# Three units in place of two at the opening of each stage, and the norm's factor a unit later

## The chip, the cores and the metric

The kernel runs on one core of a Trainium2 chip, as one launch. The metric is device time in microseconds (us), lower is better. Before the change it took 1333.68 us, the median of three runs (1332.94 to 1336.54).

## The reference

A sequence of 256 positions with 1024 features goes through two blocks. The first has a conditioned feed-forward layer (SwiGLU, 2816 wide), a mixer (a gated convolution and a two-directional gated delta rule with 8 heads) and a second SwiGLU. The second has differential attention, a squared-ReLU MLP (4096 wide), an mLSTM layer and another MLP. Each of these layers begins with the same step, and that is where the change is made:

```
def _rmsnorm(x, w):
    xf = x.astype(jnp.float32)
    y = xf * lax.rsqrt(jnp.mean(xf * xf, axis=-1, keepdims=True) + EPS)
    return (y * w.astype(jnp.float32)).astype(x.dtype)
...
        u = _modulate(_rmsnorm(h, norm_mix[l]), sh2, sc2)
        h = h + g2 * _hybrid_mixer(u, w_in[l], ...)
...
        h = h + mix.astype(h.dtype)
        h = h + sqrelu_mlp(rmsnorm(h, mlp_norm[layer]), mlp_w1[layer], mlp_w2[layer]).astype(h.dtype)
```

The norm's factor (one number per position) can be multiplied into a product behind the matrix product, so the product can start before the factor is known.

## The kernel before

**Units.** Activations lie features by positions: x and h are eight tiles of 128 x 256 (k = 0 to 7). Every float32 product is made as three: a value is split into a rounded part (hi) and a rest (lo), and hi*hi, hi*lo and lo*hi are added (`mm3`, lines 429 to 431: weights hi by x hi, weights hi by x lo, weights lo by x hi). 128 columns of weights are a *unit*: 8 tiles by 3, 24 matmuls (`unit_cols`). A stage is a row of such units, each with an accumulator in one of PSUM's eight banks: four have the tag "up", four the tag "acc", and each tag is handed out in turn.

**Weights.** `Stream` loads two units at a time from memory ("raw"). A unit is prepared by a cast on ScalarE (ACT), "whi", line 320, and a subtraction on VectorE (DVE), "wlo", line 323 (a few on GpSimd). It lies in a buffer until the last matmul that reads it; there are three such buffers in ffn1's end and the mixer (`NSLOT`), and five in all later stages (`wider`). `unit` takes the next prepared unit, prepares others into what buffers are free, and then lets side work go one step further: `flush` runs what was put off with `later`, `tick` takes one step in each generator of `self.side`.

**A stage's opening.** The last product of a stage updates h from four acc banks, pair of tiles by pair (lines 874 and 878); `x_late` makes the x of the next stage from it (hi on ACT, line 739, lo on DVE, line 743). As the pairs come one by one, `unit_first` opens two units together: for each pair the hi products of both (lines 466 and 467), then the lo products of both (line 470). Their accumulators are two acc banks. In five of the six openings an acc bank has been taken for a square of h in between (line 644), so these are the second and third bank that h is updated from.

**The norm.** `group` is called behind each unit with its evacuation. The squares are summed by matmuls (line 672) inside the unit that follows the second group (`SUM`), and DVE makes the factor from that by a row of small operations (lines 675 and 523 to 537). At the fourth group (`SPREAD`) TensorE spreads it over the partitions (line 699), ACT copies it ("rs", line 713), and all evacuations held until then run on DVE: line 1642 in the mixer ("zs", with "lbias", line 772), 945 to 957 in ffn2, 1197 in attention, 997 and 999 in the MLPs ("t", "r"), 1943 in the mLSTM ("raw"). Until then the accumulators of those units stay in their banks.

**The shifted x.** The mixer's first eight units and ffn2's first ten use an x without the conditioning's shift and without the factor ("xw"). Meanwhile `x_full`, a side job, makes the full x for the rest: per tile a multiplication on DVE ("xt", line 757), ACT's addition of the shift ("xh", line 760) and the rest on DVE ("xl", line 764). It begins when the factor is there and takes a group of tiles at each tick: pairs in the mixer; one, one and then pairs in ffn2.

**The mLSTM.** Behind the fourth unit the gates' small product (lines 2020 to 2023) takes an up bank of its own, and `ml_gates` multiplies it by the factor (lines 1808 and 1809). In attention `cores` starts the first pair of heads when its q and k are there.

What stands in the program in which order on each engine follows from the order in which this code is run; nothing reorders it later.

Of the kernel before, what the change touches and what calls it, by code (L numbers as in the profile page):

```python
# [25 lines left out]
NFF = DFF // P  # L26
NFF2 = DFF2 // P
NLATE2 = 10
SUM, SPREAD = 2, 4
NLATE = 8  # L30
SX = S + 2
FIRST = ((0, 4), (4, 8))
# [357 lines left out]
class Kern:  # L390
# [62 lines left out]

    def unit_first(self, name, x):

        w = [self.st.next(name, 0) for i in range(2)]
        self.flush()
        self.tick()
        n = x[0].shape[-1]
        pss = [self.acc2().rearrange("p a b -> p (a b)")[:, :n] for i in range(2)]  # L460
        t = self.nc.tensor
        for j in range(KT // 2):
            ks = [(k, slice(k * P, (k + 1) * P)) for k in (2 * j, 2 * j + 1)]
            for (wh, wl), ps in zip(w, pss):
                for k, s in ks:
                    t.matmul(ps, lhsT=wh[:, s], rhs=x[0][:, k], start=k == 0, stop=False, skip_group_check=True)  # L466
                    t.matmul(ps, lhsT=wl[:, s], rhs=x[0][:, k], start=False, stop=False, skip_group_check=True)  # L467
            for (wh, wl), ps in zip(w, pss):
                for k, s in ks:
                    t.matmul(ps, lhsT=wh[:, s], rhs=x[1][:, k], start=False, stop=k == KT - 1, skip_group_check=True)  # L470
        return pss
# [426 lines left out]
    def swiglu(self, nm, gate_v, late, wide=None, after_wide=None, first=None):  # L898

        nc = self.nc  # L900
        up, dn = f"w_{nm}_up", f"w_{nm}_down"
        g = {}
        with ExitStack() as es:
            fp = es.enter_context(self.tc.tile_pool(name=nm, bufs=2))
            if first is None:
                self.down_start()

            def product(n, a, b):
                gf = fp.tile([P, S], F32, tag="gf", name="gf", bufs=4)
                a(gf)  # L910
                b(gf)
                gh = fp.tile([P, S], F32R, tag="gh", name="gh", bufs=8 if first else 6)
                gl = fp.tile([P, S], F32R, tag="gl", name="gl", bufs=8 if first else 6)
                self.split(gf, gh, gl)
                g[n] = (gh, gl)

            def silu(ps):
                sa = fp.tile([P, S], F32, tag="sa", name="sa", bufs=3)
                nc.scalar.activation(sa, ps, AF.Silu)  # L919
                return sa  # L920

            def whole(n, sa, ps):
                product(n, lambda gf: None, lambda gf: nc.vector.tensor_tensor(gf, ps, sa, op=ALU.mult))  # L923

            n0 = 0
            if first is not None:
                n0 = NFIRST
                self.first_products(lambda n, a, b: whole(n, silu(a), b))
                first.close()
                self.st.widen_until(lambda nm, n: es.enter_context(self.tc.tile_pool(name=nm, bufs=n)), self.st.nfirst)  # L930
                self.down_start()
                for n in range(0, NFIRST - 3, 2):
                    self.down(dn, None, n == 0, False, [g.pop(n), g.pop(n + 1)])
            for n in range(n0, NFF):
                if wide is not None and 2 * n < NLATE2:
                    if n == 0:
                        pa, pb = self.unit_first(up, wide)
                    else:
                        pa = self.up(SX)
                        self.unit_cols(pa, up, wide)  # L940
                    sa = fp.tile([P, S], F32, tag="sa", name="sa", bufs=3)

                    def gate_a(pa=pa, sa=sa):
                        t = fp.tile([P, S], F32, tag="ta", name="ta", bufs=2)
                        nc.vector.tensor_tensor(t, pa[:, :S], self.rs, op=ALU.mult)
                        nc.scalar.activation(sa, t, AF.Silu, bias=self.late_bias(pa))
                    self.group(gate_a)
                    if n > 0:
                        pb = self.up(SX)
                        self.unit_cols(pb, up, wide)  # L950

                    def gate_b(pb=pb, sa=sa, n=n):
                        def a(gf):
                            nc.vector.tensor_tensor(gf, pb[:, :S], self.rs, op=ALU.mult)

                        def b(gf):
                            nc.vector.scalar_tensor_tensor(gf, gf, self.late_bias(pb), sa, op0=ALU.add, op1=ALU.mult)
                        product(n, a, b)
                    if 2 * n + 2 == NLATE2:
                        self.flush()  # L960
                    self.group(gate_b)
                    if 2 * n + 2 == NLATE2:
                        after_wide()
                else:
                    x = (self.xh, self.xl)
                    ps = self.up()
                    self.unit_cols(ps, up, x)
                    sa = silu(ps)
                    ps = self.up()
                    self.unit_cols(ps, up, x)  # L970
                    whole(n, sa, ps)
                if n % 2 == 1 and n >= 3:
                    self.down(dn, None, n == 3 and n0 == 0, False, [g.pop(n - 3), g.pop(n - 2)])
            gate = self.small.tile([P, KT], F32, tag="gate", name="gate")
            nc.vector.tensor_scalar(gate, self.mod(gate_v), 0.5, None, op0=ALU.mult)
            self.down(dn, None, False, True, [g.pop(NFF - 2), g.pop(NFF - 1)], self.end_step(gate, late()))

    def mlp(self, l, late):
# [4 lines left out]
        with ExitStack() as es:  # L983
            fp = es.enter_context(self.tc.tile_pool(name=f"mlp{l}", bufs=2))
            self.late()
            started = False
            first = self.unit_first(up, x)
            for n in range(NFF2):
                if n < 2:
                    ps = first[n]  # L990
                else:
                    ps = self.up()
                    self.unit_cols(ps, up, x)

                def evac(n=n, src=ps):
                    t = fp.tile([P, S], F32, tag="t", name="t")
                    nc.vector.tensor_tensor(t, src, self.rs, op=ALU.mult)  # L997
                    r = fp.tile([P, S], F32, tag="r", name="r", bufs=6)
                    nc.vector.scalar_tensor_tensor(r, t, 0.0, t, op0=ALU.max, op1=ALU.mult)
                    gh = fp.tile([P, S], F32R, tag="gh", name="gh", bufs=10)  # L1000
                    gl = fp.tile([P, S], F32R, tag="gl", name="gl", bufs=10)
                    self.split(r, gh, gl)
                    g[n] = (gh, gl)
                self.group(evac)
                if n % 2 == 1 and n >= 7:
                    if not started:
                        self.down_start()
                    self.down(dn, None, not started, False, [g.pop(n - 7), g.pop(n - 6)])
                    started = True
            for n in (NFF2 - 6, NFF2 - 4):  # L1010
                self.down(dn, None, False, False, [g.pop(n), g.pop(n + 1)])
            self.down(dn, None, False, True, [g.pop(NFF2 - 2), g.pop(NFF2 - 1)], self.end_step(None, late()))
# [148 lines left out]
    def attention(self, late):  # L1161
        nc = self.nc
        x = (self.xh, self.xl)
        with ExitStack() as es:
# [13 lines left out]

            def cores():
                for hp in range(4):  # L1180
                    while not waiting:
                        yield
                    self.side.append(self.attn_core(*waiting.popleft(), bank))
                    for _ in range(APART):
# [436 lines left out]
    def mixer(self, wide, wide_es, late):  # L1621
        nc = self.nc
        nm = "w_in"
        with ExitStack() as es:
# [4 lines left out]
            self.eps = mp.tile([P, 1], F32, name="eps")  # L1629
            nc.vector.memset(self.eps, EPS)  # L1630
            self.late()
            self.side.append(self.x_full(self.gain_mix, self.mod(3), ((0, 1), (2, 3), (4, 5), (6, 7))))
            first = self.unit_first(nm, wide)
            for n in range(NLATE):
                if n < 2:
                    ps = first[n]
                else:
                    ps = self.up(SX)
                    self.unit_cols(ps, nm, wide)
# [159 lines left out]
    def ml_gates(self, ps):  # L1799
# [5 lines left out]
        ax = mp.tile([4, S], F32, name="gax")  # L1805
        z = mp.tile([4, S], F32, name="gz")
        b_if = self.vec("b_if")
        v.tensor_tensor(gi, ps[0:4], self.rs[0:4], op=ALU.mult)
        v.tensor_tensor(gf, ps[32:36], self.rs[32:36], op=ALU.mult)
        v.tensor_scalar(gi, gi, b_if[0:4, 0:1], None, op0=ALU.add)  # L1810
# [117 lines left out]
    def mlstm(self, late):  # L1928
# [3 lines left out]
        with ExitStack() as es:  # L1932
# [77 lines left out]
            first = self.unit_first(nm, x)  # L2010
            for n in range(8):
                h, i = divmod(n, 2)
                if n < 2:
                    ps = first[n]
                else:
                    ps = self.up()
# [60 lines left out]
    def run(self):  # L2077
# [107 lines left out]
        for i, name in enumerate(st):  # L2185
# [10 lines left out]
                self.mixer(self.xw, wes, late)  # L2196
            elif name == "ffn2":
                self.late()
                self.side.append(self.x_full(self.gain_mix, self.mod(6), ((0,), (1,), (2, 3), (4, 5), (6, 7))))

                def after_wide():
                    wes.close()
# [87 lines left out]
```

## Time and profile before

| | |
|---|---|
| runs of the kernel | 1333.68 us (1332.94, 1333.68, 1336.54) |
| the profiled execution's own time | 1331.56 us |
| its span, first to last instruction | 1329.7 us |
| mean granted TensorE clock | 0.991 of full speed |
| busy: TensorE, its weight loads, DVE, ACT, GpSimd | 98%, 96%, 73%, 50%, 4% |
| waits of TensorE at the openings (line 466) | 2.4 us in 5 waits |

PE is TensorE's matmuls, PEld its weight loads, SP the engine that issues the weight loads from memory. A row of a timeline gives the start in us from the span's start, the length in us, the engine, the line in the kernel, the operation, out<-in by the program's names, the shape, and how many in a row were merged; at the end in brackets the idle time in front and what ended it. Matmuls are pipelined: one lasts 0.28 us, and the next starts 0.12 us after it. The openings lie at 209.4 (mixer), 526.5 (ffn2), 718.3 (attention), 835.3 (first MLP), 1019.7 (mLSTM) and 1132.3 us (second MLP).

### The profile page before, as it was taken

Reading aid. Unit: us, or ns where it says so; the run is one execution under the profiler, and the core shown is the slowest. Engines: PE = TensorE matmul, PEld = TensorE weight load, DVE = VectorE, ACT = ScalarE, POOL = GpSimd, SP = SyncE. Lnnn points to the kernel's source line nnn. Section 1 sums busy time; section 2 is a strip of 40 time slices with the busy share of each in tenths; the row PEclk is TensorE's granted clock in tenths of the full one; section 3 lists DMA queues with packets and bytes.
Section 4 is the critical chain, followed back from the end, with each engine's and each line's share of the span. In section 5 each row is a group of like instructions: output and inputs, shape, how many; then the busy total and the mean of one; then the engine's idle time right before and its main releaser. Section 6 shows DMA issues by size and latency. Waiting matters only on the chain.

```text
span 1329.7 us, 26472 instructions
## 1 busy us (share of the span) xinstructions
PE 1297.0 (98%) x11058; PEld 1280.2 (96%) x11058; DVE 975.8 (73%) x1831; ACT 666.8 (50%) x1096; POOL 53.1 (4%) x42
## 2 busy tenths in 40 slices
PE   8999999989999989999999999999999999999997
PEld 7999999989999989999999999999999999999997
DVE  7997768789997586966556986965667957966654
ACT  3544445657545345634445566644445654644442
POOL 0000000233020000010000000000000000000000
PEclk8999999999999989999999999999999999999998
DMA  9998862444444364587554444455554435455550
GB/s 374 345 363 311 308 254 101 158 162 156 159 133 158 130 243 164 181 294 266 188 179 145 159 156 129 167 192 187 191 191 160 154 132 188 160 183 177 186 186 32
DMA packets 36680, 255.98 MB, mean 193 GB/s; under 512 B 4336, under 2 KB 4600, under 8 KB 6096
## 3 DMA queue, kind: packets, MB, share of 16 engines
q1 hardware_dynamic: 35136, 251.47, 53.1%
q0 software_dynamic: 560, 1.44, 0.4%
q8 instruction: 86, 1.41, 0.4%
q10 hardware_dynamic: 864, 1.38, 0.3%
q14 instruction: 34, 0.28, 0.1%
HBM read 253.03 MB, written 1.25 MB: 191 GB/s over the span
## 4 chain that ended last, share of the span: by engine, by line
PE 84%; DVE 13%; issue 1%; ACT 1%; DMA 1%; SPq 0%; DVEq 0%; ACTq 0%
PE up L429 16%; PE up L431 16%; PE up L430 15%; PE acc L430 9%; PE acc L429 9%; PE acc L431 9%; DVE wlo L323 3%; DVE raw L553 2%; PE acc L466 1%; PE acc L470 1%; PE acc L1567 1%; PE acc L467 1%; DVE tmp L1450 1%; DVE x L1452 1%; DMA vecs<-in_vecs 1%
## 5 line engine op out<-in xcount | busy, mean ns | idle before, releaser
L320 ACT CAST whi<-raw 128x1024 fp32r<-128x1024 f32 x404 | 420.5, 1047 | 417.8 <-PE up L430 172.6
L323 DVE TENSOR_TENSOR wlo<-raw,whi 128x1024 fp32r<-128x1024 f32 x390 | 474.0, 1225 | 61.0 <-ACT whi L320 59.5
L429 PE MATMUL up<-xh,whi 128*128 128x256 f32 x1744 | 498.7, 286 | 0.0
L431 PE MATMUL up<-xh,wlo 128*128 128x256 f32 x1744 | 492.8, 283 | 2.0 <-DVE wlo L323 2.0
L430 PE MATMUL up<-xl,whi 128*128 128x256 f32 x1744 | 492.6, 282 | 0.0
L431 PEld LDWEIGHTS up<-xh,wlo 128*128 128x128 f32 x1744 | 333.2, 191 | 2.9 <-DVE wlo L323 2.8
L429 PEld LDWEIGHTS up<-xh,whi 128*128 128x128 f32 x1744 | 334.4, 192 | 1.4
L430 PEld LDWEIGHTS up<-xl,whi 128*128 128x128 f32 x1744 | 333.3, 191 | 0.6 <-DVE xl L764 0.2
L429 PE MATMUL acc<-gh,whi 128*128 128x256 f32 x864 | 244.0, 282 | 0.0
L431 PE MATMUL acc<-gh,wlo 128*128 128x256 f32 x864 | 243.9, 282 | 0.0
L430 PE MATMUL acc<-gl,whi 128*128 128x256 f32 x864 | 243.9, 282 | 0.0
L429 PEld LDWEIGHTS acc<-gh,whi 128*128 128x128 f32 x864 | 165.9, 192 | 0.6 <-issue 0.6
L430 PEld LDWEIGHTS acc<-gl,whi 128*128 128x128 f32 x864 | 164.6, 191 | 0.0
L431 PEld LDWEIGHTS acc<-gh,wlo 128*128 128x128 f32 x864 | 164.6, 191 | 0.0
L997 DVE TENSOR_TENSOR t<-up,rs 128x256 f32<-128x256 f32 x60 | 25.4, 423 | 102.0 <-PE up L431 102.0
L553 DVE SCALAR_TENSOR_TENSOR raw<-raw,crow 128x1024 f32<-128x1024 f32 x72 | 87.9, 1249 | 3.8 <-DMA raw<-in_stream 3.8
L923 DVE TENSOR_TENSOR gf<-up,sa 128x256 f32<-128x256 f32 x35 | 14.6, 423 | 70.6 <-PE up L431 70.6
L323 POOL TENSOR_TENSOR wlo<-raw,whi 128x1024 fp32r<-128x1024 f32 x14 | 34.5, 2463 | 286.3 <-ACT whi L320 286.3
L919 ACT ACTIVATE sa<-up 128x256 f32<-128x256 f32 x35 | 13.1, 382 | 48.6 <-PE up L431 45.1
L429 PE MATMUL up<-whi,xh 128*128 128x256 f32 x128 | 37.3, 291 | 0.2 <-DVE raw L1943 0.2
L429 PE MATMUL acc<-yh,whi 128*128 128x256 f32 x128 | 36.2, 283 | 0.0
L430 PE MATMUL up<-wlo,xh 128*128 128x256 f32 x128 | 36.0, 281 | 0.0
(490 smaller groups left out, 1842.8 us busy)
## 6 DMA issues: line engine op xcount, KB each, us to landing
raw<-in_stream SPq DMA_DIRECT2D x238, 1024.0 KB, 4.9
h<-in_x SPq DMA_DIRECT2D x2, 512.0 KB, 4.7
bias<-bdram POOLq DMA_DIRECT2D x8, 128.0 KB, 6.0
out_h<-h SPq DMA_DIRECT2D x2, 256.0 KB, 2.7
out_h<-h ACTq DMA_DIRECT2D x2, 256.0 KB, 2.9
consts<-in_consts ACTq DMA_DIRECT2D x1, 384.0 KB, 7.7
vecs<-in_vecs SPq DMA_DIRECT2D x1, 312.0 KB, 7.5
wg<-in_w_g ACTq DMA_DIRECT2D x1, 256.0 KB, 2.6
```

Of the source, the lines that this page charges most:

```text
L320: nc.scalar.copy(hi[:, :n], raw)
L323: self.lows.append(lambda: eng.tensor_tensor(lo[:, :n], raw, hi[:, :n].bitcast(F32), op=ALU.subtract))
L429: t.matmul(ps, lhsT=wh, rhs=xh, start=start, stop=False, skip_group_check=True)
L430: t.matmul(ps, lhsT=wh, rhs=xl, start=False, stop=False, skip_group_check=True)
L431: t.matmul(ps, lhsT=wl, rhs=xh, start=False, stop=stop, skip_group_check=True)
L466: t.matmul(ps, lhsT=wh[:, s], rhs=x[0][:, k], start=k == 0, stop=False, skip_group_check=True)
L467: t.matmul(ps, lhsT=wl[:, s], rhs=x[0][:, k], start=False, stop=False, skip_group_check=True)
L470: t.matmul(ps, lhsT=wh[:, s], rhs=x[1][:, k], start=False, stop=k == KT - 1, skip_group_check=True)
L553: self.nc.vector.scalar_tensor_tensor(w, w, 1.0, self.crow, op0=ALU.mult, op1=ALU.mult, accum_out=self.mods[:, c:c + 1])
L923: product(n, lambda gf: None, lambda gf: nc.vector.tensor_tensor(gf, ps, sa, op=ALU.mult))
L997: nc.vector.tensor_tensor(t, src, self.rs, op=ALU.mult)
L1450: v.tensor_tensor(tt, m[:, j + 1:, j:j + 1].to_broadcast([P, n, w]), x[:, j:j + 1, :w].to_broadcast([P, n, w]), op=ALU.mult)
```

## The change

`unit_first` takes three units; the third has an up bank, not an acc bank, and stands behind the other two in each of the block's loops. The stages use its third result. The spread moves from the fourth group to the fifth. As the gates of the mLSTM and the first core of attention now may be reached before the factor is there, they wait for it by ticks. `x_full` makes three, three and two tiles in the mixer and four pairs in ffn2.

```
-SUM, SPREAD = 2, 4
+SUM, SPREAD = 2, 5
...
     def unit_first(self, name, x):
-        w = [self.st.next(name, 0) for i in range(2)]
+        w = [self.st.next(name, 0) for i in range(3)]
         self.flush()
         self.tick()
         n = x[0].shape[-1]
-        pss = [self.acc2().rearrange("p a b -> p (a b)")[:, :n] for i in range(2)]
+        pss = [self.acc2().rearrange("p a b -> p (a b)")[:, :n] for i in range(2)] + [self.up(n)]
...
                     if n == 0:
-                        pa, pb = self.unit_first(up, wide)
+                        pa, pb, pc = self.unit_first(up, wide)
+                    elif n == 1:
+                        pa = pc
...
-                if n < 2:
+                if n < 3:
                     ps = first[n]
...
-                    while not waiting:
+                    while not waiting or not self.normed():
                         yield
...
-            self.side.append(self.x_full(self.gain_mix, self.mod(3), ((0, 1), (2, 3), (4, 5), (6, 7))))
+            self.side.append(self.x_full(self.gain_mix, self.mod(3), ((0, 1, 2), (3, 4, 5), (6, 7))))
...
         b_if = self.vec("b_if")
+        while not self.normed():
+            yield
...
-                self.side.append(self.x_full(self.gain_mix, self.mod(6), ((0,), (1,), (2, 3), (4, 5), (6, 7))))
+                self.side.append(self.x_full(self.gain_mix, self.mod(6), ((0, 1), (2, 3), (4, 5), (6, 7))))
```

How it moves instructions, at three places. First TensorE at the mixer's opening, one pair of x's tiles (xwh its hi part, xwl its lo part; acc and up are accumulators, whi and wlo a unit's weights):

```order
 L466 MATMUL acc<-xwh,whi 128x258
 L467 MATMUL acc<-xwh,wlo 128x258
+L466 MATMUL up<-xwh,whi 128x258
+L467 MATMUL up<-xwh,wlo 128x258
+L466 MATMUL up<-xwh,whi 128x258
+L467 MATMUL up<-xwh,wlo 128x258
 L470 MATMUL acc<-xwl,whi 128x258 x4
+L470 MATMUL up<-xwl,whi 128x258 x2
 L466 MATMUL acc<-xwh,whi 128x258
 L467 MATMUL acc<-xwh,wlo 128x258
```

The third unit's four hi products stand behind those of the second, and its two lo products behind the four others; a pair has 18 matmuls where it had 12.

Second DVE in the mixer behind the spread, from the first group of the shifted x on, before:

```order
L757 SCALAR_TENSOR_TENSOR xt<-h,gain_2437,rs 128x256 x2
L1642 TENSOR_TENSOR zs<-up,rs 128x256
L772 COPY lbias<-up 128x1
L323 TENSOR_TENSOR wlo<-raw,whi 128x1024
L489 TENSOR_TENSOR wb<-wba,wb 128x256
L764 SCALAR_TENSOR_TENSOR xl<-xt,mods,xh 128x256 x2
L757 SCALAR_TENSOR_TENSOR xt<-h,gain_2437,rs 128x256 x2
L1642 TENSOR_TENSOR zs<-up,rs 128x256
L772 COPY lbias<-up 128x1
L323 TENSOR_TENSOR wlo<-raw,whi 128x1024
L764 SCALAR_TENSOR_TENSOR xl<-xt,mods,xh 128x256 x2
```

And of the changed kernel, where line 1642 has become 1644:

```order
L757 SCALAR_TENSOR_TENSOR xt<-h,gain_2437,rs 128x256 x3
L1644 TENSOR_TENSOR zs<-up,rs 128x256
L772 COPY lbias<-up 128x1
L323 TENSOR_TENSOR wlo<-raw,whi 128x1024
L764 SCALAR_TENSOR_TENSOR xl<-xt,mods,xh 128x256 x3
L757 SCALAR_TENSOR_TENSOR xt<-h,gain_2437,rs 128x256 x3
L1644 TENSOR_TENSOR zs<-up,rs 128x256
L772 COPY lbias<-up 128x1
L323 TENSOR_TENSOR wlo<-raw,whi 128x1024
L764 SCALAR_TENSOR_TENSOR xl<-xt,mods,xh 128x256 x3
```

The first group stands behind five evacuations instead of four, and between two subtractions for the weights there are six instructions of x where there were four. In front of the norm's evacuation (line 675), where one subtraction stood, there are two.

Third TensorE at the spread in the mLSTM (the number behind a name tells one buffer from another; wgh and wgl are the gates' weights), before:

```order
L429 MATMUL up_12568<-xh_12349,whi_12436 128x256
L430 MATMUL up_12568<-xl_12350,whi_12436 128x256
L431 MATMUL up_12568<-xh_12349,wlo_12437 128x256
L699 MATMUL acc_12598<-consts_87,rtok_12547 128x128 x2
L429 MATMUL up_12615<-xh_12349,wgh_10227 64x256
L430 MATMUL up_12615<-xl_12350,wgh_10227 64x256
L431 MATMUL up_12615<-xh_12349,wgl_10228 64x256
```

And of the changed kernel:

```order
L429 MATMUL up_12623<-xh_12349,whi_12441 128x256
L430 MATMUL up_12623<-xl_12350,whi_12441 128x256
L431 MATMUL up_12623<-xh_12349,wlo_12442 128x256
L699 MATMUL acc_12658<-consts_87,rtok_12576 128x128 x2
L429 MATMUL up_12678<-xh_12349,whi_12537 128x256
L430 MATMUL up_12678<-xl_12350,whi_12537 128x256
L431 MATMUL up_12678<-xh_12349,wlo_12538 128x256
```

Behind the spread stood the gates' product; now a full unit stands there, the sixth of the stage, and the gates' product has come in front of the fifth.

## Rows read from the trace of the kernel before

**Rows 1.** The page's first part, the busy time of each engine:

```profile
PE 1297.0 (98%) x11058; PEld 1280.2 (96%) x11058; DVE 975.8 (73%) x1831; ACT 666.8 (50%) x1096; POOL 53.1 (4%) x42
```

**Rows 2.** Waits of PE: whom it waited for, us in total, times, longest:

```profile
PE acc L466 <- DVE h L878: 1.5, 2, 0.8
PE acc L1112 <- ACT v L1205: 1.2, 3, 0.8
...
PE acc L466 <- DVE h L874: 0.9, 3, 0.3
```

**Rows 3.** Timeline of the mixer's opening, 209 to 219 us:

```profile
210.78 0.39 PE L466 MATMUL acc<-xwh,whi 128*128 128x258 f32 x1 [0.69 <-DVE h L878]
...
215.70 0.64 PE L470 MATMUL acc<-xwl,whi 128*128 128x258 f32 x4
216.13 2.00 ACT L320 CAST whi<-raw 128x1024 fp32r<-128x1024 f32 x2 [2.27 <-PE acc L470]
216.18 0.28 PE L429 MATMUL up<-xwh,whi 128*128 128x258 f32 x1
...
217.22 1.23 DVE L323 TENSOR_TENSOR wlo<-raw,whi 128x1024 fp32r<-128x1024 f32 x1 [0.68 <-ACT whi L320]
218.68 0.50 PE L672 MATMUL acc<-ones,ssum 128*128 128x1 f32 x4
```

**Rows 4.** Timeline of the mixer behind it, 219 to 239 us:

```profile
219.21 0.16 DVE L675 TENSOR_SCALAR nm<-acc 128x2 f32<-128x2 f32 x1 [0.77 <-PE acc L672]
...
221.38 2.36 DVE L323 TENSOR_TENSOR wlo<-raw,whi 128x1024 fp32r<-128x1024 f32 x2
...
237.62 1.22 DVE L323 TENSOR_TENSOR wlo<-raw,whi 128x1024 fp32r<-128x1024 f32 x1
238.89 0.39 PE L431 MATMUL up<-xh,wlo 128*128 128x256 f32 x1 [0.79 <-DVE wlo L323]
```

**Rows 5.** Timeline of ffn2 from the spread on:

```profile
539.65 0.60 PE L699 MATMUL acc<-consts,rtok 128*128 128x128 f32 x4
540.68 1.28 ACT L946 ACT_TABLE_LOAD   x1
...
542.52 0.48 DVE L957 SCALAR_TENSOR_TENSOR gf<-gf,lbias,sa 128x256 f32<-128x256 f32 x1 [0.33 <-ACT sa L946]
...
543.26 0.15 DVE L772 COPY lbias<-up 128x1 f32<-128x1 f32 x1
```

**Rows 6.** Timeline of the first MLP from the spread on:

```profile
847.84 0.60 PE L699 MATMUL acc<-consts,rtok 128*128 128x128 f32 x4
...
851.07 0.42 DVE L997 TENSOR_TENSOR t<-up,rs 128x256 f32<-128x256 f32 x1
```

**Rows 7.** Timeline of the mLSTM from the spread on:

```profile
1032.24 0.60 PE L699 MATMUL acc<-consts,rtok 128*128 128x128 f32 x4
1032.60 0.36 PE L429 MATMUL up<-xh,wgh 128*64 128x256 f32 x1
1032.88 0.38 ACT L713 COPY rs<-acc 128x256 f32<-128x256 f32 x1 [2.34 <-PE acc L699]
...
1034.50 0.75 DVE L1943 TENSOR_TENSOR raw<-up,rs 128x256 f32<-128x256 f32 x2
```

**Rows 8.** Stretches: us, PE, PEld, DVE, ACT, POOL busy (count), PE clock, DMA share, GB/s:

```profile
471.00:474.00 3.00, 1.53 (x7) 1.36 (x8) 3.00 (x7) 1.49 (x2) 0.00 (x0) 0.72 0.02 8
474.00:477.00 3.00, 3.00 (x16) 3.00 (x16) 2.97 (x5) 0.00 (x0) 0.00 (x0) 0.50 0.41 112
477.00:480.00 3.00, 3.00 (x19) 3.00 (x19) 2.06 (x4) 1.30 (x2) 0.00 (x0) 0.64 0.99 412
294.00:300.00 6.00, 4.12 (x31) 4.05 (x32) 6.00 (x17) 1.35 (x5) 3.00 (x1) 1.00 0.70 254
```

**Rows 9.** Timeline of PE, two waits in the mixer:

```profile
295.88 1.10 PE L1305 MATMUL acc<-k 128*128 128x256 f32 x4 [2.56 <-DVE L L1311]
...
471.57 0.36 PE L429 MATMUL up<-yah,whi 128*128 128x256 f32 x1 [2.75 <-ACT whi L320]
```

More of the change, by code (lines that the diff above doesn't have):

```diff
@@ L1631, in mixer @@
             self.late()
-            self.side.append(self.x_full(self.gain_mix, self.mod(3), ((0, 1), (2, 3), (4, 5), (6, 7))))
+            self.side.append(self.x_full(self.gain_mix, self.mod(3), ((0, 1, 2), (3, 4, 5), (6, 7))))
             first = self.unit_first(nm, wide)
             for n in range(NLATE):
-                if n < 2:
+                if n < 3:
                     ps = first[n]
@@ L2012, in mlstm @@
                 h, i = divmod(n, 2)
-                if n < 2:
+                if n < 3:
                     ps = first[n]
```

## The prediction

> **What bounds the kernel now.** First the page's busy table: TensorE (PE) has work in 98% of the span and VectorE (DVE) in 73% [rows 1]. A time can fall only where PE waits, and rises wherever a new wait is put in front of it. So second the view of waits on PE [rows 2]: the openings of the stages (line 466) waited for DVE twice for 1.5 us together and three times for 0.9 us together, and no row of that view has an opening waiting for a pair of x's tiles. That is all a third open unit could fill. Third the timeline at one opening, the mixer's [rows 3]. Unit 0's first four matmuls run, then PE waits 0.69 us for "h L878". The pair of x's tiles is the one unit 0 has just used; what is missing is unit 1's accumulator bank, which h's update must empty. From then on there is no wait up to 216.18: two units use 12 matmuls a pair, 1.44 us at the 0.12 us from matmul to matmul (215.70 to 216.18 is four of them; 216.18 to 218.68 is 21), and x keeps up.
>
> Below, units of a stage are counted from 0, a unit is 24 matmuls or 2.88 us, and "the spread" is line 699.
>
> **The change, part by part.** *Three units open.* No matmul is added or removed. The order puts unit 2's matmuls behind those of unit 1, so the wait at unit 1's bank stays where it is: gain 0. The other end of that estimate is all five waits gone: 2.4 us [rows 2] and about 0.2 us of slower restart each (210.78 took 0.39 us where others take 0.28, and the next came 0.11 late): 3.4 us. I take 0. Unit 2's weights are ready before the opening in every stage (in the mixer ACT has no weight cast between h's update and 216.13), so its earlier turn costs nothing.
>
> *The mixer's weight buffers.* This stage alone has three weight buffers; all others have five. All three are now held until the block ends, and unit 3's cast (ACT, line 320) must wait for unit 0's last matmul. Before, the same cast waited too (216.13, ended by "acc L470"), but behind it PE had unit 2 to do. After: the block ends at 216.18 + 2.88 = 219.06; its last six matmuls are line 470, unit 0's two first, so the cast starts about 0.3 us before, at 218.77. One cast is 1.00 us (2.00 for two): 219.8. Its subtraction on DVE is 1.23 us: 221.05 [rows 3]. Unit 3's third matmul needs it; due at 219.30 it starts at 221.1. With the restart that is 2.0 us of new wait.
>
> *The mixer's DVE queue.* Behind the norm DVE has more to do than PE gives it time for: from 221.4, when the factor is ready, to 238.84, when unit 9's subtraction ends, it is idle for some 0.5 us, and PE waits for that subtraction (238.89) [rows 4]. After: the factor's sum (line 672) comes 19 matmuls behind unit 3's third, 223.5; its evacuation 0.53 us later, the factor 2.2 us after that (219.21 to 221.4): 226.3. From there the same work is ahead of DVE less one subtraction (two, not one, now stand before the norm): 17.4 - 1.15 = 16.2, less up to 0.4 of the old idle time, so unit 9's subtraction ends at 242.1 to 242.5 and PE goes on at 242.2 instead of 238.89: 3.3 us, in which the 2.0 and the old 0.95 are contained. The bounds: if the x work were hidden, 2.0 - 0.95 = 1.05; if the waits that I find one by one, at units 7 (0.3), 8 (1.2 and 0.5) and 9 (1.3), all add up, 2.0 + 3.3 - 0.95 = 4.35. I take 3.3, since the queue's length is read from rows. Groups of three x tiles keep the work and save one round trip to ACT.
>
> *The spread a unit later: banks.* There are four "up" banks. Now units 2, 3 and 4 are in three of them when the spread comes, unit 5 takes the fourth and unit 6 needs unit 2's. It is due at the spread + 0.36 + 2.88 = 3.24 us. When is unit 2's bank read? In ffn2 unit 2 is third in DVE's queue, behind a multiplication that waits for ACT's table load: 543.26 + 0.15 is 3.76 us behind the spread, and the table load does not move: 0.5 us of wait, bounds 0.2 and 0.7 [rows 5]. In the two MLPs the third "t" ends at 851.07 + 0.42, which is 3.65 behind [rows 6]; there DVE can be 0.35 earlier since it no longer has a subtraction in front of the norm's evacuation when that is due: 0.1 to 0.4, I take 0.25 each. In the mixer and in attention the third read is one instruction and comes in time: 0 (bound 0.3 each).
>
> *The mLSTM.* Here the gates' product (line 2023) takes a fourth up bank between units 3 and 4, so all four are full at the spread and the very next unit, 5, needs unit 2's. The spread is released to ACT 0.64 us after it starts, ACT copies for 0.38 (to 1033.26), then three reads of 0.33 us pitch, the last ending 0.42 after its start: 1.02 + 0.67 + 0.42 = 2.1 us behind the spread, while PE arrives 0.36 behind it: 1.75 us [rows 7]. DVE has longer than before to finish the subtractions, since the gates' product now lies ahead of the spread, so nothing else delays it. I take 1.7; bounds 1.4, if 0.3 of it is given back at a later wait of the stage, and 2.9, if one more subtraction (1.2) stands in front of the reads.
>
> *The rest.* Attention's first core starts one tick later; its products stand between others and only move: 0, bounds -0.3 and +0.5, since three waits there for ACT's copies of v, 1.2 us together, may come out otherwise [rows 2]. The mLSTM gates run a tick later; what follows them is not late.
>
> **The sum.** 3.3 + 0.5 + 0.25 + 0.25 + 1.7 = 6.0 us; the bounds add to 2.5 (1.05 + 0.2 + 0.1 + 0.1 + 1.4 - 0.3) and 9.8 (4.35 + 0.7 + 0.4 + 0.4 + 2.9 + 0.5 + 0.6). The profiled execution took 1331.56 us, 1.9 more than its span, and the median of the runs is 2.1 above it. So 1337.6 by the profiled one and 1339.7 by the median. A measurement of this kernel can tell about 0.3%, 4.0 us, from no change: slower begins at 1337.7, faster ends at 1329.7.
>
> **The rivals.** *The waits lie beside others: no change to speak of.* If DVE catches up in the mixer and the banks of the MLPs are read early, what is left is about 1 in the mixer and 1.4 in the mLSTM: 1336.1. For it: DVE is free in 27% of the span; against it: not in the two stretches in question.
>
> *Faster.* The third unit fills the waits at the openings (-3.4), and the shifted x, made in three groups, is done before unit 9 asks (-0.95): 1329.3. It decides if PE has unit 2's matmuls to issue while unit 1's bank is not free, or if the cast of unit 3 finds a free buffer. Against it are the order and the three buffers.
>
> *The clock falls too.* A wait of 2.75 us for a cast in the mixer's last third, and a shorter one for the subtraction behind it, were followed by a granted clock of 0.50, that is 1.2 GHz, in 474 to 477 us, where 16 matmuls fill 3 us [rows 8, 9]. With 0.72 and 0.64 on both sides of it that is 3.4 us of clock lost in 9 us; less what fell into the waits themselves, about 2.5. A wait of 2.56 us for DVE at 295.88 left the clock at 1.00 [rows 8, 9]. The new wait in the mixer is 1.8 us with only two matmuls inside, that in the mLSTM 1.75: nearer to the second. If one of them brings the clock down: 1342.2, if both do, 1344.7. The Trainium skill ("TensorE: Matmul & The Clock Gate", section "A second HAM failure mode: psum-queue depth-cycling") says that a kernel which cycles its groups of matmuls through PSUM banks can pause so often in between that the clock swings between its levels. By that rule the bank waits that the change adds would cost more than their length in every stage; the mean granted clock is 0.991 (the table of the profile) over a span in which every unit takes another bank, so I give it no more than the waits' rows do.
>
> **How the numbers follow.** Chances: the forecast 0.59 (alone 1336.5 to 1342, and four in five of it above 1337.7), no change to speak of 0.22, clock 0.12, faster 0.07. Slower: 0.48 + 0.12 = 0.60; same: 0.11 + 0.22 = 0.33; faster 0.07. The range, 1334 to 1343.5, leaves out most of the faster case and half of the clock's.
>
> **What would show it.** In the mixer: line 429 of unit 3 waiting for ACT's cast and line 431 for its subtraction, together 1.8 us, and further waits for "wlo" in units 7 to 9. In the mLSTM: the first matmul behind the spread waiting 1.7 us for "raw". In ffn2 and the MLPs: the second unit behind the spread waiting a few tenths for "lbias" or "t". At the openings: the same five waits for "h". I am wrong if unit 3 of the mixer starts without a wait, if the waits at line 466 are gone, or if PE's granted clock falls anywhere that it did not before.

## The result and the profile after

The changed kernel took 1340.68 us (median of six runs, 1339.71 to 1344.36), the kernel before 1333.76 us in the same comparison (six runs, 1332.21 to 1337.69). The ratio is 1.0051 with a 95% interval of 1.0039 to 1.0064: slower by 0.5%, 6.9 us where 6.0 were predicted.

The profiled execution of the changed kernel is the slowest of the six (1344.36 us, span 1342.3, granted clock 0.986); that of before (1331.56 us) lies below all six of its runs. Their difference of 12.8 us is therefore not the change alone, and the first thing to do is to cut it by stages. The table gives, from the first matmul of line 466 in one stage to that in the next (in the last row to the last spread, the kernel's last matmuls), the length of each stage in us, for two profiles of either kernel. The second ones are of the experiments b_again and a_again below.

| stage | before | before again | after | after again |
|---|---|---|---|---|
| mixer | 317.1 | 317.2 | 320.8 | 322.1 |
| ffn2 | 191.8 | 191.9 | 196.1 | 193.6 |
| attention | 117.0 | 118.5 | 118.6 | 118.5 |
| first MLP | 184.3 | 184.3 | 184.8 | 184.7 |
| mLSTM | 112.7 | 112.6 | 114.0 | 114.1 |
| second MLP | 189.6 | 189.7 | 189.8 | 189.8 |

The busy table of after shows the same work as before (the same counts, DVE 975.5 us where it was 975.8) and PE in a smaller share of a longer span [rows 1]:

```profile
PE 1304.7 (97%) x11058; PEld 1285.2 (96%) x11058; DVE 975.5 (73%) x1831; ACT 665.7 (50%) x1096; POOL 52.2 (4%) x42
```

So the time went into waits. The view of waits on PE of after (whom it waited for, us in total, times, longest) answers [rows 2]:

```profile
PE up L431 <- DVE wlo L323: 4.9, 8, 0.8
PE up L429 <- ACT whi L320: 4.0, 3, 2.5
...
PE up L429 <- DVE raw L1947: 1.7, 1, 1.7
...
PE acc L466 <- DVE h L878: 1.5, 2, 0.8
PE acc L1114 <- ACT v L1207: 1.2, 3, 0.8
...
PE acc L466 <- DVE h L874: 0.9, 3, 0.3
...
PE up L429 <- DVE lbias L772: 0.4, 1, 0.4
```

The five waits of the openings are what they were, 1.5 and 0.9 us, and so are the three for v. Three waits for a cast stand where one stood before, the wait for "lbias" is new, and the one for "raw" is 1.7 us where before had one of 0.2 us, at a later unit. The timeline of after shows where, one row for each new wait that the prediction spoke of or missed, and for two of them the row that they are read against:

```profile
211.63 0.39 PE L466 MATMUL acc<-xwh,whi 128*128 128x258 f32 x1 [0.69 <-DVE h L878]
...
219.64 2.94 ACT L320 CAST whi<-raw 128x1024 fp32r<-128x1024 f32 x3 [4.92 <-PE acc L470]
220.74 0.39 PE L429 MATMUL up<-xwh,whi 128*128 128x258 f32 x1 [0.66 <-ACT whi L320]
222.00 0.39 PE L431 MATMUL up<-xwh,wlo 128*128 128x258 f32 x1 [0.75 <-DVE wlo L323]
...
224.40 0.50 PE L672 MATMUL acc<-ones,ssum 128*128 128x1 f32 x4
...
238.46 0.39 PE L431 MATMUL up<-xh,wlo 128*128 128x256 f32 x1 [0.76 <-DVE wlo L323]
...
243.04 0.38 PE L431 MATMUL up<-xh,wlo 128*128 128x256 f32 x1 [0.79 <-DVE wlo L323]
...
550.99 0.36 PE L429 MATMUL up<-xwh,whi 128*128 128x258 f32 x1 [0.43 <-DVE lbias L772]
...
604.45 0.39 PE L429 MATMUL up<-xh,whi 128*128 128x256 f32 x1 [0.81 <-ACT whi L320]
...
605.71 0.39 PE L431 MATMUL up<-xh,wlo 128*128 128x256 f32 x1 [0.75 <-DVE wlo L323]
...
864.20 0.28 PE L431 MATMUL up<-xh,wlo 128*128 128x256 f32 x1
864.62 0.36 PE L429 MATMUL up<-xh,whi 128*128 128x256 f32 x1
...
1050.79 0.36 PE L429 MATMUL up<-xh,whi 128*128 128x256 f32 x1 [1.67 <-DVE raw L1947]
```

Read against [rows 3, 4]: the opening's wait is again 0.69 us; unit 3 now waits 0.66 for its cast, whose own idle time ended at "acc L470", the block's end, and 0.75 for its subtraction; unit 9's third matmul comes 31.41 us behind the opening's wait (243.04 - 211.63) where it came 28.11 behind (238.89 - 210.78). That is the mixer's 3.3. The norm's sum (line 672) comes 12.77 us behind the opening's wait; the wait at 238.46 is unit 8's. The row at 864.62 has no wait named, but it starts 0.42 us behind the row before it instead of 0.12: 0.30 lost, which the prediction puts down to a bank (up_bank_second, below, tests it). The rows at 604.45 and 605.71 were in no step of the prediction.

The mean clock hides one more thing, so the stretches are read (columns as in [rows 8]). Of after, behind the ffn2 wait and in attention, then of before at the same distance behind the openings:

```profile
606.00:609.00 3.00, 3.00 (x17) 3.00 (x17) 3.00 (x4) 2.08 (x3) 0.00 (x0) 0.53 0.96 314
609.00:612.00 3.00, 3.00 (x25) 3.00 (x25) 3.00 (x5) 0.00 (x0) 0.00 (x0) 0.90 1.00 407
...
741.00:744.00 3.00, 3.00 (x23) 3.00 (x23) 1.81 (x11) 1.05 (x1) 0.00 (x0) 0.79 0.50 210
744.00:747.00 3.00, 3.00 (x19) 3.00 (x19) 2.76 (x5) 0.00 (x0) 0.00 (x0) 0.64 0.29 41
```

```profile
600.00:603.00 3.00, 3.00 (x27) 3.00 (x27) 3.00 (x6) 0.19 (x1) 0.00 (x0) 1.00 0.86 298
603.00:606.00 3.00, 3.00 (x27) 3.00 (x27) 1.87 (x4) 1.68 (x4) 0.00 (x0) 1.00 1.00 407
...
732.00:735.00 3.00, 3.00 (x28) 3.00 (x27) 2.85 (x7) 0.94 (x3) 0.00 (x0) 1.00 0.59 249
735.00:738.00 3.00, 3.00 (x27) 2.78 (x26) 2.26 (x7) 1.51 (x2) 0.00 (x0) 1.00 0.58 156
```

The granted clock fell towards 1.2 GHz in two places where the first profile of before has it at 1.00. At 3 us times one less the clock, the first took 1.7 us (1.41 + 0.30) and the second 1.7.

### The profile page after: what moved, and what is told of

Read it like the earlier page. It is cut to its first block, busy times and chain, and to the rows that moved or that the text cites. A ratio compares the mean times of both kernels' runs of the same rounds, so it can differ in the third digit from the quotient of the medians.

```text
span 1342.3 us, 26456 instructions
## 1 busy us (share of the span) xinstructions
PE 1304.7 (97%) x11058; PEld 1285.2 (96%) x11058; DVE 975.5 (73%) x1831; ACT 665.7 (50%) x1096; POOL 52.2 (4%) x42
## 4 chain that ended last, share of the span: by engine, by line
PE 81%; DVE 14%; ACT 2%; issue 2%; DMA 2%; SPq 0%; DVEq 0%; ACTq 0%
PE up L429 15%; PE up L431 14%; PE up L430 14%; PE acc L430 9%; PE acc L429 9%; PE acc L431 9%; DVE wlo L323 4%; DVE raw L553 2%; DMA raw<-in_stream 1%; PE acc L466 1%; PE acc L470 1%; PE acc L1569 1%; PE acc L467 1%; DVE tmp L1452 1%; ACT whi L320 1%
## 5 line engine op out<-in xcount | busy, mean ns | idle before, releaser
L429 PE MATMUL up<-xh,whi 128*128 128x256 f32 x1712 | 491.7, 287 | 2.7 <-DVE raw L1947 1.7
L431 PE MATMUL up<-xh,wlo 128*128 128x256 f32 x1712 | 485.5, 284 | 3.5 <-DVE wlo L323 3.5
L430 PE MATMUL up<-xl,whi 128*128 128x256 f32 x1712 | 485.1, 283 | 0.6 <-issue 0.4
L429 PEld LDWEIGHTS up<-xh,whi 128*128 128x128 f32 x1712 | 329.8, 193 | 4.9 <-ACT whi L320 2.9
L431 PEld LDWEIGHTS up<-xh,wlo 128*128 128x128 f32 x1712 | 328.4, 192 | 4.7 <-DVE wlo L323 4.7
L430 PEld LDWEIGHTS up<-xl,whi 128*128 128x128 f32 x1712 | 328.7, 192 | 1.5 <-issue 0.6
```

The lines of the kernel that those rows point to most:

```text
L429: t.matmul(ps, lhsT=wh, rhs=xh, start=start, stop=False, skip_group_check=True)
L430: t.matmul(ps, lhsT=wh, rhs=xl, start=False, stop=False, skip_group_check=True)
L431: t.matmul(ps, lhsT=wl, rhs=xh, start=False, stop=stop, skip_group_check=True)
```

## The experiments

**The changed kernel and the kernel before, once more.** Nothing is edited; what is wanted is a second profile of each.

> The changed kernel once more, with a new profile. In the first profile a load of weights in ffn2 (near 604 us) came 12.8 us after it was issued, PE waited 1.9 us for its cast and subtraction, and the granted clock was 0.57 in the 4 us behind. Theory: that wait is of that execution and no part of the change: the new profile has no wait for a cast in ffn2 behind the bias transfers, the span is 3 to 5 us shorter, and the median is again 6 to 8 us above the kernel before. Rival: the change itself brings the load late (weights asked for earlier meet the bias transfers): the wait and the clock's fall are there again at the same place.

Measured: 1341.87 us (five runs, 1339.35 to 1344.14), ratio 1.0062 (1.0049 to 1.0075). The theory of a single bad execution fell: 73.6 us behind the opening of ffn2 PE again waited for a subtraction (0.75 us long; 0.92 lost, counted from the start of one matmul to the start of the next). All seven profiles of this case in which ffn2 is the changed one and its bias transfers were not held back have a wait there, 0.35 to 2.5 us lost. The rival held for the wait; the clock's fall behind it is a matter of the execution: two of the seven have it.

> The kernel before once more, for a second profile. In five profiles the granted clock of attention's first 20 us fell to about a half for 3 to 5 us in the four whose mixer opens later than before and in neither of the two whose mixer is as before; attention itself is the same in five of the six. Theory (which execution has this fall is chance, given by where the stage falls in time): it may or may not be in this profile, in one stage or another, and the stages without a fall are as long as before within 0.2 us: 112.65 in the mLSTM, 184.3 and 189.6 in the MLPs, 191.8 in ffn2, where no wait for a cast stands 73 us behind the opening. Rival (ffn2's late load and attention's fall are luck alone): one of them is here too.

Measured: one run of 1333.84 us. Its ffn2 has no such wait and is 191.9 us long, but its attention is 118.5: of the rival's two, attention's fall is here and the late load is not. Stretches of this second profile of before, in the mixer and in attention:

```profile
294.00:297.00 3.00, 0.70 (x3) 0.68 (x4) 3.00 (x8) 0.29 (x1) 2.76 (x2) 0.99 0.27 38
297.00:300.00 3.00, 3.00 (x14) 2.82 (x14) 3.00 (x9) 1.23 (x4) 0.42 (x1) 0.50 0.99 418
...
729.00:732.00 3.00, 3.00 (x22) 3.00 (x22) 2.14 (x8) 1.04 (x2) 0.00 (x0) 0.74 0.50 137
732.00:735.00 3.00, 3.00 (x20) 3.00 (x20) 2.73 (x11) 0.61 (x1) 0.00 (x0) 0.70 0.69 292
```

Attention's fall is in the kernel before too, so it is not the change's; it was missing in the first profile. And the wait of 2.56 us that left the clock at 1.00 in [rows 8, 9] is here again, 2.56 us long, with the clock at 0.50 behind it. One kernel, one wait, two outcomes; the wait stands in all 13 profiles of this case, and a fall follows it at once in eight.

**The mixer as before.**

```
-            self.late()
-            ...x_full(..., ((0, 1, 2), (3, 4, 5), (6, 7)))
-            first = self.unit_first(nm, wide)
+            self.late(4)
+            ...x_full(..., ((0, 1), (2, 3), (4, 5), (6, 7)))
+            first = self.unit_first(nm, wide, 2)
...
-                if n < 3:
+                if n < 2:
```

> The changed kernel, but the mixer opens two units, spreads after four groups and shifts x in pairs, as before the change. Theory (the mixer costs 3.3 of the change's 7): 3.3 us faster than the changed kernel, and the waits at the mixer's opening and in units 7 to 9 are those of before: unit 9's third matmul 28.1 us behind the opening in place of 31.4. Rival (the mixer's waits are given back later or lie beside the loads that it waits for anyway): under 1.5 us faster.

Measured: 1339.72 us (ratio 1.0046, 1.0032 to 1.0060), 2.2 us below the changed kernel of the same comparison (1341.87). The runs alone do not tell 3.3 from 1.5. The timeline does: unit 9's third matmul is at 28.11 us behind the opening's wait at 210.96.

```profile
239.07 0.39 PE L431 MATMUL up<-xh,wlo 128*128 128x256 f32 x1 [0.79 <-DVE wlo L323]
...
461.52 2.02 PE L1600 MATMUL acc<-dg,o 128*128 128x128 f32 x16 [1.54 <-DVE dg L706]
```

The rival (given back later) needs a second place, near the stage's end. The row for "dg" is 250.56 us behind the opening's wait here, and 250.57 in before. In the profile of gates_behind_spread (below), whose mixer is the changed one and whose clock fell as often up to there, it is 253.84 behind the wait at 210.96:

```profile
464.80 2.02 PE L1600 MATMUL acc<-dg,o 128*128 128x128 f32 x16 [1.53 <-DVE dg L706]
```

So the 3.3 stays to the end, and the rival falls.

**The mixer with two units and the late spread.** As the experiment above, with `late()` and the groups of three kept.

> The changed kernel with only two units open in the mixer; the spread stays after the fifth group and x is shifted in the larger groups. Theory (the new wait at unit 3 is the three weight buffers, 2.0 us; the rest of 3.3 is VectorE's queue behind the late spread): no wait for a cast at unit 3; the spread still comes 2.9 us later than before with one more subtraction done ahead of it, so unit 9's subtraction is 1.3 to 1.7 us later than before and the kernel 1.6 to 2.0 us faster than the changed one. Rival A (buffers alone): all 3.3 come back. Rival B (the late spread alone sets the end of the queue): nothing comes back, within 0.5 us.

Measured: 1339.96 us (1.0046, 1.0033 to 1.0059). Unit 3 starts without a wait, and unit 9's third matmul comes at 29.34 behind the opening's wait at 211.38:

```profile
240.72 0.39 PE L431 MATMUL up<-xh,wlo 128*128 128x256 f32 x1 [0.79 <-DVE wlo L323]
```

That is 2.07 us earlier than in the changed kernel and 1.23 later than before (1.3 to 1.7 was expected): both causes are real, the three buffers with 2.1 and the late spread (with the larger groups), through DVE's queue, with 1.2. Both rivals fall, since neither all nor nothing came back.

**The gates' product behind the spread.**

```
-                if n == 3:
+                if n == 4:
                     wgh, wgl = self.wg
```

> The changed kernel with the mLSTM gates' product one unit later, behind the spread in place of ahead of it. Theory (unit 5 waits because the gates' product takes the fourth up bank before the spread): the wait of 1.7 us behind the spread is gone, 1.4 to 1.8 us faster than the changed kernel. Rival (VectorE reads the banks late whatever stands in the fourth): the wait comes back one unit later, under 0.5 us faster.

Measured: 1338.57 us (1.0040, 1.0027 to 1.0052), 3.3 below a_again's median, with wide intervals. The mLSTM is 112.1 us long in place of 114.0 and 114.1, and no wait is left behind the spread: the fourth bank was the cause, and moving its user gave 1.9 to 2.0, a little more than the wait itself (1.67, 1.79 lost).

**The bias transfers later.** First by 12 more `yield` ahead of the eight transfers in `bias_job`, then, since that moved nothing, ahead of the product whose result they carry:

```
-        yield
-        yield
+        for _ in range(14):
+            yield
         ps = self.ps_up.tile([P, 384], F32, tag="up", name="up")
```

> The changed kernel, but the eight transfers of the attention bias start 12 units later in ffn2. In all five profiles with the changed ffn2, PE waited 0.35 to 1.9 us for a cast or its subtraction 73 us behind the opening, where the kernel before has no wait; the bias transfers began 1.5 to 2 us later behind the opening than before, beside a load of weights. Theory (the load shares the transfer engines with the bias and lands too late): the wait is gone and ffn2 is 192.4 to 192.6 us long, 191.84 and the bank's 0.6; the kernel is 0.4 to 1.9 us faster than the changed one, if the bias does not meet another late load. Rival (the weights' stream alone is late there, since three units take one weight more at the opening): the wait stays.

Measured: 1342.91 us (1.0063, 1.0050 to 1.0076). It did not test what it was meant to. The timeline of POOL and PE shows the transfers at 584.60, 55.0 us behind the opening at 529.58, as in a_again without the edit (54.3 in after), and the waits in place:

```profile
584.60 4.18 POOL L1039 DMA_DIRECT2D bias<-bdram  x8 [5.77 <-DMA bdram<-brows]
...
603.53 0.39 PE L429 MATMUL up<-xh,whi 128*128 128x256 f32 x1 [1.40 <-ACT whi L320]
...
604.79 0.39 PE L431 MATMUL up<-xh,wlo 128*128 128x256 f32 x1 [0.76 <-DVE wlo L323]
```

The transfers, placed 12 units later in the program, start no later here: GpSimd had been idle for 5.77 us in front of them, and what ended that is the row in brackets, the data that they carry. So this is in effect one more measurement of the changed kernel, 9.0 us above before.

> The changed kernel, with the small product that makes the attention bias 12 units later on PE, so that the bias transfers, which need its result, really start some 36 us later. (Putting them later in the program alone left them where they were, 55 us behind ffn2's opening, since nothing else stands in GpSimd's queue; the wait for the cast stayed.) Theory: without the bias beside it the load lands in time, no wait 72 to 75 us behind the opening, ffn2 192.4 us long, 1 to 2 us faster than the changed kernel. Rival (the weights' stream alone is late, or the bias meets the next late load): the wait of 1 to 2.4 us stays or stands elsewhere in ffn2.

Measured: 1339.08 us (1.0038, 1.0025 to 1.0050). Now the transfers start 86.8 us behind the opening, the waits for cast and subtraction are gone, and ffn2 is 192.3 us long, as expected (192.4). The kernel is 4.8 us above before (3.3 to 6.7 by the interval).

```profile
616.48 4.17 POOL L1038 DMA_DIRECT2D bias<-bdram  x8 [5.95 <-DMA bdram<-brows]
```

The view of the tile "raw" (the weights from memory) gives for each kernel the shortest, median and longest time from issue to landing, here between 54 and 74 us behind ffn2's opening: first after, then with the bias held back, then before.

```profile
DMA to landing us min/median/max: 4.7/10.9/12.8
```

```profile
DMA to landing us min/median/max: 4.8/5.2/6.8
```

```profile
DMA to landing us min/median/max: 5.0/8.9/10.1
```

In the changed kernel a load beside the bias takes twice as long. The Trainium skill ("DMA: Bandwidth & Descriptors", section "Issuing engines are not separate DMA queues") says that transfers started from the scalar, sync or gpsimd engine run on the same 16 transfer engines and interleave; these rows agree. Before, too, the loads met the bias (10.1), but landed in time. In after the transfers begin 54.3 us behind the opening, before 52.9, and the loads take up to 2.7 us longer. Over all profiles without the hold the four with the ffn2 of before have them at 52.9 to 53.4 and no wait, the seven with the changed one at 54.0 to 55.1 and a wait. Why a shift of 1.4 us costs that much is not settled; that no wait is left without the bias is shown.

**The up bank for the second unit, three units open.** One line behind the list of banks in `unit_first`:

```
+        pss.insert(1, pss.pop())
```

> The changed kernel with the third accumulator (an up bank) given to the second unit and the second acc bank to the third, so that the unit whose bank h's update frees last comes third. Theory (the openings wait for unit 1's bank, not for x): the five waits of 0.27 to 0.77 us there shrink by 0.48 each, to at most 0.3; and since the bank that is used again first is now read second, the waits behind the spread in ffn2 (0.6), the MLPs (0.30, 0.24) and the mLSTM (1.79) shrink by about 0.35 each: 2.5 to 3.3 us faster than the changed kernel. Rival (x or the next cast is what is late at the openings): the waits move to the next pair and under 1 us is gained, all of it behind the spread.

Measured: 1337.69 us (1.0029, 1.0019 to 1.0040), 3.0 below the changed kernel's first median and 4.2 below a_again's. In ffn2 the opening's wait is 0.29 in place of 0.77, in the mixer 0.20 in place of 0.69, in the last three stages there is none. Behind the spread, ffn2 and the MLPs have no wait; the mLSTM has 1.34, now put down to a cast. From its timeline (the added line makes line 466 of the others its line 467):

```profile
529.28 0.39 PE L467 MATMUL acc<-xwh,whi 128*128 128x258 f32 x1 [0.29 <-DVE h L879]
...
1044.63 0.36 PE L429 MATMUL up<-xh,whi 128*128 128x256 f32 x1 [1.34 <-ACT whi L320]
```

The openings had waited for a bank of h's update, and x does keep up. Whether the 1.34 is the cast or still a bank is not settled: the gates' product stands in the fourth bank here too.

**The kernel before with unit 1 in an up bank.**

```
-        pss = [self.acc2()... for i in range(2)]
+        pss = [self.acc2()..., self.up(n)]
```

and the gates' product as above.

> The kernel before (two units open, spread after four) with unit 1's accumulator in an up bank, and the mLSTM gates' product one unit later, behind the spread. Theory: no unit waits for a bank of h's update any more, so the five opening waits (0.44 to 0.93 us each with the slower restart, 3.1 together) go; behind the spread the first up bank used again is the second one read: at most 0.3 us in ffn2, nothing elsewhere. 2.5 to 3.2 us faster than before. Rival (x comes just in time and the wait moves from the bank to x): under 1 us.

Measured: 1333.64 us, ratio 0.9993 (0.9984 to 1.0002): no change that can be told. All five opening waits are gone, and four came back a few us later, at the matmuls that sum the squares; two of them in the timeline:

```profile
537.11 0.60 PE L672 MATMUL acc<-ones,ssum 128*128 128x1 f32 x4 [0.87 <-DVE ssum L658]
...
846.89 0.35 PE L672 MATMUL acc<-ones,ssum 128*128 128x1 f32 x2 [0.34 <-DVE ssum L658]
```

My theory fell, and the rival has the size right but not the cause, since x is not what is waited for. The mixer is an exception, where the sum comes in time and 0.9 us are gained at unit 9 (its third matmul comes 28.52 us behind the stage's first matmul, where it was 29.44); this profile's mixer is no shorter as a whole, 317.4 us, with the clock lower over more of it. With two units open the sum sits one unit earlier than with three, and there the opening's wait had covered it.

**By stage.** Each stage with what the runs showed to be the better of the two:

```
-        pss = [self.acc2()... for i in range(2)] + [self.up(n)]
+        pss = [self.acc2()... for i in range(nu - 1)]
+        pss.insert(1, self.up(n))
...
-                        pa, pb, pc = self.unit_first(up, wide)
-                    elif n == 1:
-                        pa = pc
+                        pa, pb = self.unit_first(up, wide, 2)
...
-                self.late()
-                ...x_full(..., ((0, 1), (2, 3), (4, 5), (6, 7)))
+                self.late(4)
+                ...x_full(..., ((0,), (1,), (2, 3), (4, 5), (6, 7)))
```

with the mixer and the gates' product edited as above; attention, the MLPs and the mLSTM keep three units.

> By stage: mixer and ffn2 open two units and spread after four groups as before, unit 1 in an up bank; attention, the MLPs and the mLSTM open three units and spread after five, with an acc bank, an up bank and an acc bank in this order; the mLSTM gates' product behind the spread. Theory (from the stage lengths measured: mixer -0.9, ffn2 0, MLPs -0.4 and -0.6, mLSTM -0.9 against before): 2.5 to 3.0 us faster than before, 1330.9. Rival (what is taken away at the openings comes back behind them, as at the norm's sum): within 1 us of before.

Measured: 1330.6 us (six runs, 1329.0 to 1333.86) against 1334.29, ratio 0.9974 (0.9961 to 0.9987): 3.7 us below the kernel before. The MLPs are 183.9 and 189.0 us long and the mLSTM 111.6.

> The by-stage kernel, but ffn2 also opens three units in the order acc, up, acc and spreads after five, with the bias product 12 units later as well. Theory: ffn2 has neither the bank's wait nor the cast's, and an opening wait 0.48 shorter than before: 0.3 to 0.5 us faster than the by-stage kernel. Rival (the cast's wait stays): 0.9 to 2 us slower than it.

Measured: 1330.2 us (eight runs), ratio 0.9969 (0.9958 to 0.9979). ffn2 is 191.2 us long where the by-stage kernel has 191.9, 0.7 gained where 0.3 to 0.5 was expected. The two cannot be told apart by their medians. Both are faster than either kernel of the case, by 0.3% against before.

## Why the prediction was right, and where not

**Three units, gain 0: right.** The five opening waits stood unchanged, and up_bank_second showed the reason, the order of the banks.

**The mixer, 3.3: right, with its parts.** Unit 3 waited 0.66 and 0.75 us; with the slow start of each row and of the next matmul 1.95 were lost, where 2.0 was said. The norm's sum came 12.77 us behind the opening's wait (12.72 said, 223.5 less 210.78), and unit 9 was 3.3 late. Of the waits named one by one, which made the upper bound, unit 7 had none and unit 8 had 0.76 and 0.13 us where 1.2 and 0.5 were said: that bound was too high. The experiment with two units divides this into 2.1 for the buffers and 1.2 for the spread. The groups of three were not tried apart from the late spread. a_again's mixer is 1.3 longer still: it has a fall of the clock at 297 to 303 us that the first profile of after lacks.

**Banks in ffn2 and the MLPs, 0.5 and 0.25 each: right.** Lost at the row: 0.60, 0.30 and 0.24. up_bank_second, where another bank comes first, has none of the three.

**The mLSTM, 1.7: right in mechanism, the wait itself 1.67.** The stage grew by 1.4 to 1.5 only, since a wait of 0.17 us (0.33 lost) at a later unit of before is gone; the lower bound had allowed for such a return.

**Missing from the sum: ffn2's late load.** The prediction said of the earlier weights that their turn "costs nothing", and stopped at PE and ACT. It did not follow the queues in ffn2: the bias transfers moved against the loads, and a load that had landed just in time came late. That is a sixth term of 0.4 to 2.5 us, seen in seven profiles and removed by bias_held. With 1 to 2 us for it the steps add to 7 to 8, and the changed kernel was measured 6.9, 8.2 and (bias_later) 9.0 above before. With that term away, bias_held was 4.8 above before, and its interval holds the 6.0. So it is partly luck that 6.0 lies so near the first 6.9: a whole term was missing.

**The clock: the forecast held, but not for its reason.** No profile has a fall behind the new waits of the mixer or the mLSTM. Yet the sign "if the granted clock falls anywhere that it did not before" came true, and misled: attention's fall is in either kernel, and only the one behind ffn2's wait, in two of seven profiles, belongs to the change. The argument that a wait of 2.56 us leaves the clock up rested on a single execution; the second profile of before refutes it. The Trainium skill ("TensorE: Matmul & The Clock Gate", section "What's actually happening") says of a kernel's cold start that the monitor's window runs free, so that the same kernel pays differently from run to run. The traces agree as far as one wait had two outcomes; the window itself no run here shows. In the section "A second HAM failure mode: psum-queue depth-cycling" the page tells of another kernel, in which cycling through PSUM banks made the clock swing. Nothing of that shows here: no profile has a fall behind a bank's wait at an opening or at the spread, and the mean clock of the changed kernel's runs was 0.985 to 0.990 (11 runs), that of before 0.987 to 0.991 (the nine runs compared with the last five of those).

**What stays open:** how much of 6.9 us is the chance of clock falls, the size of ffn2's term from run to run and why so small a shift of the transfers brings it, and how the mixer's 1.2 divides between the late spread and the groups of three.

## What to carry to other kernels

Before a wait is taken away, look at what it covers: the wait at the opening hid the norm's sum, and removing it alone gave nothing in the MLPs (184.35 us for 184.33 in the first), while removing it with the sum one unit later gave 0.4 and 0.6 us there. When a step moves by a microsecond or two, follow the transfers of every queue in that stage: a load that lands just in time leaves no row in a list of waits, so its lack of slack does not show there. And before a wait or its absence is blamed on the clock, take a second profile of the same kernel.

## What was not expected of the hardware

The same wait of 2.56 us was followed by a granted clock of 1.00 in one execution of a kernel and 0.50 in another. Loads of 1024 KB that land in about 5 us alone took up to 12.8 us in after, and 13.4 in bias_later, beside eight transfers of 128 KB each. And at the 32 small matmuls that sum attention's norm (line 686, two columns each, 3.6 us together in after) the clock fell in 11 of the 13 profiles of this case, behind them or, in two, while they still ran, in stretches in which PE counts as fully busy; that these matmuls bring the fall was not tested.
